# Two blocks of a 2048-wide model on one Trainium2 core: gate and up products with tokens stationary

## The chip, the core and the metric

The program runs on one core of one Trainium2 chip. The metric is the device time of one execution, in microseconds (us). Before the change the median of three runs is 2844.01 us (2843.94 to 2844.36). The core's engines work side by side, each through its own list of instructions in order, and wait for each other by semaphores: TensorE (matrix products, called PE in the profile; its weight loads are PEld), VectorE (DVE), ScalarE (ACT), GpSimd (POOL), and SyncE (SP), whose queue issues the transfers of weights.

## The reference

Two residual blocks follow each other, for 256 tokens of 2048 features, all in float32. The first has a modulation computed from a vector, a mixer with sliding-window attention and a gated linear recurrence, and a feed-forward layer. The second has gated linear attention and a feed-forward layer. What matters here are the two feed-forward layers, with 5632 hidden features:

```python
# first block
h2 = modulate(rms_norm(x, norm2_g[l]), sh2, sc2)
gate, up = jnp.split(h2 @ w_ffn_in[l], 2, axis=-1)
x = x + g2 * ((jax.nn.silu(gate) * up) @ w_ffn_out[l])
...
# second block
def swiglu(h, w_gu, w_down):
    g, u = jnp.split(h @ w_gu, 2, axis=-1)
    return (jax.nn.silu(g) * u) @ w_down
...
x = x + swiglu(rms_norm_2(x, norm_g[i, 1]), ffn_w_gu[i], ffn_w_down[i])
```

## The kernel before

Activations live in SBUF with features on the 128 partitions and the 256 tokens along the free axis: a tile of four feature tiles is `[128, 4, 256]`, a "slot" of 4 KB a partition, of which there are 24. The weights stream through once. A chunk is 1 MB: four k-tiles of 128 rows by 512 columns. `split` (L137) loads it on SP's queue into one of three `raw` buffers and makes, for two k-tiles at a time, a high part on ScalarE (L145, a copy to the rounded type float32r) and a low part on VectorE (L147, the difference); three buffers each hold such halves. The activations are kept as pairs of high and low parts in the same way (`split_act`, `normed`, `gained`). A product in nearly full precision is then the sum of three products: high by high, high by low, low by high.

`accumulate` (L151) does one chunk. In its usual form the weights are stationary: for each of four k-tiles and four feature tiles, three products (L169, L171, L173) with a 128x128 weight tile as the stationary operand and 256 tokens moving, 48 to a chunk; the result has features on partitions, in two PSUM banks of 512 columns. With `tokens=True` the activations are stationary: for each of four k-tiles and two token tiles, three products (L162 to L164) with a 128x128 piece of the activations stationary and 512 weight columns moving, 24 to a chunk; the result has tokens on partitions, one bank for each token tile. Before the change this second form serves the values of the attention (group 13) and those of the linear attention (`gvps`). PSUM has eight banks, handed out by the `bank` function in turn of need.

A feed-forward layer (`swiglu`, L614) works in two halves of 6 and 5 groups of 512 hidden features. For each group j: the gate product (four chunks, banks `fgps`), SiLU into a slot `sg`; then the up product (four chunks, banks `fups`), multiplied on VectorE with `sg`; then `split_act` of this into the pair `hid`. When the half is done, four groups of output features (`fops`) take the hidden pairs as moving operands, five or six chunks each, and `update` adds the result to x. In the first layer group 0 of the gate starts from `gx`, which lacks the norm's factor of each token; the factor is multiplied in after the product, and the share of the modulation's shift, `fb`, is a vector of 512 computed ahead by `matvec` (products on VectorE, a sum over partitions by four one-column products on TensorE, L226) and used as SiLU's bias. In the second layer all groups start from products without that factor: VectorE multiplies the gate by it before SiLU and again after SiLU (for the up part), L899 and L903.

The order of the work: the code is a list in which loads, conversions and products stand one behind the other, and work beside the weight stream stands in tasks (`spawn`) that go on at each `pump()`, between chunks. The conversions of chunks are marked as more urgent than what surrounds them. A scheduler takes this list with its data dependencies, and fixes for each engine an order in which an instruction goes to the engine when it is ready by the scheduler's own estimate, the one that stands earlier (or is more urgent) first. On the chip each engine keeps this order and waits where an input isn't there yet.

Of the kernel before, what the change touches and what calls it, by code (L numbers as in the profile page):

```python
# [18 lines left out]
P = 128  # L19
# [30 lines left out]
def block_pair_kernel(ctx: ExitStack, tc: tile.TileContext, a: dict):  # L50
# [20 lines left out]

    def halves(t):
        return [t[:, 0:2, :], t[:, 2:4, :]]

# [21 lines left out]
    # A task is a generator; it resumes between chunks, after as many as it yields.  # L96
# [40 lines left out]
    def split(ap):  # L137
        """hi + lo == the chunk, two k-tiles at a time."""
# [12 lines left out]
    def accumulate(ps, ap, src, first, last, tokens=False):  # L151
        """One chunk of four k-tiles by 512 features into two banks."""
        parts = split(ap)
        xh, xl = src
        for kk in range(4):
# [3 lines left out]
            if tokens:  # L159
                for t in range(2):  # L160
                    tsl = slice(t * P, (t + 1) * P)
                    nc.tensor.matmul(ps[t], xh[:, kk, tsl], hi[:, wk, :], start=fst, stop=False)  # L162
                    nc.tensor.matmul(ps[t], xh[:, kk, tsl], lo[:, wk, :], start=False, stop=False)
                    nc.tensor.matmul(ps[t], xl[:, kk, tsl], hi[:, wk, :], start=False, stop=lst)  # L164
                continue
            for f in range(4):
                wsl = slice(f * P, (f + 1) * P)
                o = ps[f // 2][:, f % 2, :]
                nc.tensor.matmul(o, hi[:, wk, wsl], xh[:, kk, :], start=fst and f % 2 == 0,  # L169
                                 stop=False, skip_group_check=True)  # L170
                nc.tensor.matmul(o, hi[:, wk, wsl], xl[:, kk, :], start=False, stop=False,  # L171
                                 skip_group_check=True)
                nc.tensor.matmul(o, lo[:, wk, wsl], xh[:, kk, :], start=False, stop=lst,  # L173
# [20 lines left out]
    def split_act(src, name):  # L194
        hi = slot(name + "h", F32R)
        nc.scalar.activation(hi, src, AF.Copy)
        lo = slot(name + "l", F32R)
        nc.vector.tensor_tensor(lo, src, f32(hi), ALU.subtract)
        return hi, lo

# [5 lines left out]
    def matvec(srcs, col, width, done, queue=nc.gpsimd):  # L206
        """Steps of vector @ width columns; srcs[k]: the rows of the vector's k-th 128 elements."""
# [14 lines left out]
        def reduce():  # L222
            n = width // P
            ps = bank("mvp")
            for f in range(n):
                nc.tensor.matmul(ps[:, f:f + 1], state["acc"][:, f * P:(f + 1) * P],  # L226
                                 ones[:, 0:1], start=True, stop=True)
            done(ps[:, 0:n])
# [51 lines left out]
    def normed(g, gain, inv, shift, name):  # L280
        t = slot(name + "t")
        hi = slot(name + "h", F32R)
        lo = slot(name + "l", F32R)
        for f in range(4):
# [4 lines left out]
            nc.scalar.activation(hi[:, f, :], t[:, f, :], AF.Identity, bias=sh)  # L289
            nc.vector.scalar_tensor_tensor(lo[:, f, :], t[:, f, :], sh, f32(hi[:, f, :]),  # L290
                                           ALU.add, ALU.subtract)
        return hi, lo

    def gained(g, gain, name):
        """hi, lo of gain * x; the norm's per-token factor is applied after the product."""
        hi = slot(name + "h", F32R)
        lo = slot(name + "l", F32R)
        for f in range(4):
            gj = gain[:, 4 * g + f:4 * g + f + 1]
            nc.scalar.activation(hi[:, f, :], x[g][:, f, :], AF.Copy, scale=gj)  # L300
            nc.vector.scalar_tensor_tensor(lo[:, f, :], x[g][:, f, :], gj, f32(hi[:, f, :]),
                                           ALU.mult, ALU.subtract)
        return hi, lo
# [4 lines left out]
    # ======================== first block ====================================  # L308
# [12 lines left out]
    def attend(g, q):  # L321
# [52 lines left out]
        yh = slot("yah", F32R)  # L374
        yl = slot("yal", F32R)
        for b, o in ((0, o0), (1, o1)):
            sl = slice(b * P, (b + 1) * P)
            nc.scalar.activation(yh[:, :, sl], o, AF.Copy)
            nc.vector.tensor_tensor(yl[:, :, sl], o, f32(yh[:, :, sl]), ALU.subtract)
        y_attn[g] = (yh, yl)  # L380

# [29 lines left out]
    # groups that keep their banks over all of k, and groups summed up in a slot  # L411
# [78 lines left out]
    # decay constant of the recurrence: -8 softplus(-lambda)  # L490
# [25 lines left out]
    def recur(g, ups):  # L516
# [30 lines left out]
        # 1 - a^2 = (1 + a^2) tanh(-log a)  # L547
# [45 lines left out]
    # the shift's share of the first gate group, whose norm factor comes after the product  # L593
    fb = const.tile([P, 4], F32, name="fb")
# [418 lines left out]
```

## Time and profile before

The profiled execution spans 2842.5 us from its first to its last instruction; a run's time also holds what lies around the span.

| | before |
|---|---|
| median of three runs | 2844.01 us |
| span of the profiled execution | 2842.5 us |
| TensorE busy | 2795.1 us (98%) |
| VectorE busy | 1815.7 us (64%) |
| ScalarE busy | 1313.2 us (46%) |
| granted TensorE clock, mean | 1.000 |
| HBM read | 597.06 MB, 211 GB/s over the span |

How to read it: busy time is the time in which at least one instruction of the engine was under way. Products on TensorE overlap: one lasts longer than the distance to the start of the next. A group's row has the line, engine, operation, the tiles written and read, their shapes, the count, then busy us, mean ns of one, and the idle time of the engine just before them with what ended it. A row of the timeline has start and duration in us, engine, line, operation and count. A row of the waits has who waited for whom, the total, the times and the longest. A row of windows has the stretch, its length, then busy us and instructions for each engine shown, the granted clock, the share of the DMA engines and GB/s.

### The profile page before, as it was taken

Reading aid. Unit: us, or ns where it says so; the run is one execution under the profiler, and the core shown is the slowest. Engines: PE = TensorE matmul, PEld = TensorE weight load, DVE = VectorE, ACT = ScalarE, POOL = GpSimd, SP = SyncE. Lnnn points to the kernel's source line nnn. Section 1 sums busy time; section 2 is a strip of 40 time slices with the busy share of each in tenths; the row PEclk is TensorE's granted clock in tenths of the full one; section 3 lists DMA queues with packets and bytes.
Section 4 is the critical chain, followed back from the end, with each engine's and each line's share of the span. In section 5 each row is a group of like instructions: output and inputs, shape, how many; then the busy total and the mean of one; then the engine's idle time right before and its main releaser. Section 6 shows DMA issues by size and latency. Waiting matters only on the chain.

```text
span 2842.5 us, 52147 instructions
## 1 busy us (share of the span) xinstructions
PE 2795.1 (98%) x22662; PEld 2760.6 (97%) x22662; DVE 1815.7 (64%) x1998; ACT 1313.2 (46%) x1481; POOL 25.7 (1%) x52
## 2 busy tenths in 40 slices
PE   4999999999999999999999999999999999999999
PEld 4999999999999999999999999899999999999999
DVE  8887866977777865444444667866655554455554
ACT  3446438763445444333444545555444443334333
POOL 1100000000000000000000000000000000000000
PEclk9999999999999999999999999999999999999999
DMA  9974784868875865555555544444555555555554
GB/s 370 353 298 143 279 294 171 289 221 319 327 261 181 295 251 187 180 187 178 185 187 179 182 168 163 148 146 166 178 182 189 179 182 189 178 183 188 178 190 151
DMA packets 100198, 602.54 MB, mean 212 GB/s; under 512 B 11120, under 2 KB 11632, under 8 KB 40576
## 3 DMA queue, kind: packets, MB, share of 16 engines
q1 hardware_dynamic: 93056, 574.03, 57.1%
q0 software_dynamic: 6912, 25.17, 2.2%
q8 instruction: 177, 2.90, 0.4%
q14 instruction: 53, 0.43, 0.0%
HBM read 597.06 MB, written 2.10 MB: 211 GB/s over the span
## 4 chain that ended last, share of the span: by engine, by line
PE 98%; DVE 1%; issue 0%; ACT 0%; DMA 0%; SPq 0%; DVEq 0%
PE fups L169 6%; PE fgps L169 6%; PE fops L173 6%; PE fops L171 6%; PE fops L169 6%; PE fups L173 6%; PE fups L171 6%; PE fgps L173 6%; PE fgps L171 6%; PE part L169 2%; PE part L171 2%; PE part L173 2%; PE aops L169 1%; PE glps L169 1%; PE ups L169 1%; PE wops L169 1%
## 5 line engine op out<-in xcount | busy, mean ns | idle before, releaser
L147 DVE TENSOR_TENSOR lo<-raw,hi 128x1024 fp32r<-128x1024 f32 x928 | 1135.1, 1223 | 937.9 <-ACT hi L145 936.3
L145 ACT ACTIVATE hi<-raw 128x1024 fp32r<-128x1024 f32 x928 | 980.9, 1057 | 1389.5 <-PE fops L171 292.7
L169 PE MATMUL fups<-hh,hi 128*128 128x256 f32 x1408 | 398.5, 283 | 0.0
L173 PE MATMUL fups<-hh,lo 128*128 128x256 f32 x1408 | 398.5, 283 | 0.0
L169 PE MATMUL fops<-hidh,hi 128*128 128x256 f32 x1408 | 398.5, 283 | 0.0
L171 PE MATMUL fops<-hidl,hi 128*128 128x256 f32 x1408 | 398.5, 283 | 0.0
L173 PE MATMUL fops<-hidh,lo 128*128 128x256 f32 x1408 | 398.5, 283 | 0.0
L171 PE MATMUL fups<-hl,hi 128*128 128x256 f32 x1408 | 398.5, 283 | 0.0
L169 PE MATMUL fgps<-hh,hi 128*128 128x256 f32 x1344 | 380.6, 283 | 0.0
L173 PE MATMUL fgps<-hh,lo 128*128 128x256 f32 x1344 | 380.3, 283 | 0.0
L171 PE MATMUL fgps<-hl,hi 128*128 128x256 f32 x1344 | 380.3, 283 | 0.0
L171 PEld LDWEIGHTS fups<-hl,hi 128*128 128x128 f32 x1408 | 270.3, 192 | 0.0
L169 PEld LDWEIGHTS fops<-hidh,hi 128*128 128x128 f32 x1408 | 270.3, 192 | 0.0
L171 PEld LDWEIGHTS fops<-hidl,hi 128*128 128x128 f32 x1408 | 270.3, 192 | 0.0
L173 PEld LDWEIGHTS fops<-hidh,lo 128*128 128x128 f32 x1408 | 270.3, 192 | 0.0
L169 PEld LDWEIGHTS fups<-hh,hi 128*128 128x128 f32 x1408 | 270.3, 192 | 0.0
L173 PEld LDWEIGHTS fups<-hh,lo 128*128 128x128 f32 x1408 | 270.3, 192 | 0.0
L171 PEld LDWEIGHTS fgps<-hl,hi 128*128 128x128 f32 x1344 | 258.0, 192 | 0.0
L169 PEld LDWEIGHTS fgps<-hh,hi 128*128 128x128 f32 x1344 | 258.0, 192 | 0.0
L173 PEld LDWEIGHTS fgps<-hh,lo 128*128 128x128 f32 x1344 | 258.0, 192 | 0.0
L218 DVE SCALAR_TENSOR_TENSOR mva<-mvw,cact,mva 128x1024 f32<-128x1024 f32 x180 | 230.3, 1280 | 14.2 <-DMA mvw<-ada_w 12.5
L169 PE MATMUL part<-hh,hi 128*128 128x256 f32 x512 | 147.3, 288 | 0.0
(319 smaller groups left out, 5511.7 us busy)
## 6 DMA issues: line engine op xcount, KB each, us to landing
raw<-w_in SPq DMA_DIRECT2D x88, 1024.0 KB, 5.0
raw<-w_ffn_in SPq DMA_DIRECT2D x88, 1024.0 KB, 4.9
raw<-ffn_w_gu SPq DMA_DIRECT2D x88, 1024.0 KB, 4.9
mvw<-ada_w SPq DMA_DIRECT2D x144, 512.0 KB, 6.8
raw<-gla_w_in SPq DMA_DIRECT2D x48, 1024.0 KB, 4.9
raw<-w_ffn_out SPq DMA_DIRECT2D x44, 1024.0 KB, 4.9
raw<-ffn_w_down SPq DMA_DIRECT2D x44, 1024.0 KB, 4.9
mvw<-ada_w POOLq DMA_DIRECT2D x48, 512.0 KB, 8.2
```

The costliest lines, as they stand in the source:

```text
L145: nc.scalar.activation(hi, rb, AF.Copy)
L147: nc.vector.tensor_tensor(lo, rb, f32(hi), ALU.subtract)
L169: nc.tensor.matmul(o, hi[:, wk, wsl], xh[:, kk, :], start=fst and f % 2 == 0, stop=False, skip_group_check=True)
L171: nc.tensor.matmul(o, hi[:, wk, wsl], xl[:, kk, :], start=False, stop=False, skip_group_check=True)
L173: nc.tensor.matmul(o, lo[:, wk, wsl], xh[:, kk, :], start=False, stop=lst, skip_group_check=True)
L218: nc.vector.scalar_tensor_tensor(state["acc"], w, col(k), state["acc"], ALU.mult, ALU.add)
```

## The change

Gate and up products of both layers take the second form of `accumulate`: `project(..., True)`, with tokens stationary. Their results stand with tokens on partitions, so SiLU and the product with up work on `[128 tokens, 2, 512]`, and the norm's factor becomes a scalar of each partition: `by_token` transposes the row of factors and keeps one column for each token tile. In the second layer SiLU takes that factor as its scale, and the factor of the up part goes into the product of the two; in the first layer's group 0 the factor and the shift row `fb` (now `[128, 512]`, the same on all partitions, made by one 512-column product with a matrix of ones) are applied by one VectorE instruction for each token tile. The output products `fops` still need hidden features on partitions, so the task `turned` transposes the product on TensorE, eight 128x128 transposes for each group into two banks `tps`, and makes the high and low part from there. The task is spawned behind the up group with a delay that lets it go on at the very next `pump()`.

Pairs become a class: two tiles `[128, 2, 2, 256]`, each with high and low part of two feature tiles, in place of one tile of high and one of low parts; `split_act` and the attention's output write them in halves. This holds for every stage. The rest of the diff takes out comments.

```diff
+    class Pair:
+        def __init__(self, name):
+            self.t = [slot(name, F32R, [P, 2, 2, T]) for _ in range(2)]
...
+        def hi(self, kk):
+            return self.t[kk // 2][:, kk % 2, 0, :]
+        def lo(self, kk):
+            return self.t[kk // 2][:, kk % 2, 1, :]
+        def his(self, b):
+            return self.t[b][:, :, 0, :]
+        def los(self, b):
+            return self.t[b][:, :, 1, :]
...
     def split_act(src, name):
-        hi = slot(name + "h", F32R)
-        nc.scalar.activation(hi, src, AF.Copy)
-        lo = slot(name + "l", F32R)
-        nc.vector.tensor_tensor(lo, src, f32(hi), ALU.subtract)
-        return hi, lo
+        p = Pair(name)
+        for b, part in enumerate(halves(src)):
+            nc.scalar.activation(p.his(b), part, AF.Copy)
+            nc.vector.tensor_tensor(p.los(b), part, f32(p.his(b)), ALU.subtract)
+        return p
...
             ps = bank("mvp")
+            if row:
+                nc.tensor.matmul(ps[:, 0:width], ones, state["acc"], start=True, stop=True)
+                done(ps[:, 0:width])
+                return
...
+    def by_token(inv, name):
+        out = small.tile([P, 2], F32, tag="invp", name=name)
+        ps = bank("tokps", [P, T])
+        for t in range(2):
+            nc.tensor.transpose(ps[:, t * P:(t + 1) * P], inv[:, t * P:(t + 1) * P], ident)
+            nc.vector.tensor_copy(out[:, t:t + 1], ps[:, t * P:t * P + 1])
+        return out
...
-    fb = const.tile([P, 4], F32, name="fb")
+    fb = slot("fb", shape=[P, 512])
...
+    def turned(sv):
+        p = Pair("hid")
+        yield p
+        for b in range(2):
+            tp = bank("tps", [P, 2, T])
+            for i in range(2):
+                f = 2 * b + i
+                for t in range(2):
+                    nc.tensor.transpose(tp[:, i, t * P:(t + 1) * P], sv[:, t, f * P:(f + 1) * P],
+                                        ident)
+            nc.scalar.activation(p.his(b), tp, AF.Copy)
+            nc.vector.tensor_tensor(p.los(b), tp, f32(p.his(b)), ALU.subtract)
+
     def swiglu(w_in, w_out, gate, up, update):
         for n, half in enumerate((range(0, 6), range(6, FG))):
-            hid = []
+            hid, turns = [], []
             for j in half:
                 sg = gate(j)
                 pump()
-                hid.append(up(sg, j))
+                gen = turned(up(sg, j))
+                hid.append(next(gen))
+                turns.append(spawn(gen, 1))
                 pump()
             for f in range(NG):
-                update(n, f, project(chunks_of(w_out, f, list(half)), hid, "fops"))
+                chunks = chunks_of(w_out, f, list(half))
+                ps = banks("fops")
+                for c in range(len(chunks)):
+                    finish(turns[c])
+                    accumulate(ps, chunks[c], hid[c], c == 0, c == len(chunks) - 1)
+                    if c < len(chunks) - 1:
+                        pump()
+                update(n, f, ps)
                 pump()
...
+        norm2["invp"] = by_token(norm2["inv"], "invp2")
...
     def gate1(j):
-        sg = slot("sg")
-        ps = project(chunks_of("w_ffn_in", j), gx if j == 0 else h2, "fgps")
+        sg = slot("sg", shape=[P, 2, 512])
+        ps = project(chunks_of("w_ffn_in", j), gx if j == 0 else h2, "fgps", True)
         if j == 0:
             finish(norm_task)
-            for b, part in enumerate(halves(sg)):
-                nc.vector.tensor_tensor(part, ps[b], pair(norm2["inv"]), ALU.mult)
-            for f in range(4):
-                nc.scalar.activation(sg[:, f, :], sg[:, f, :], AF.Silu, bias=fb[:, f:f + 1])
+            for t in range(2):
+                nc.vector.scalar_tensor_tensor(sg[:, t, :], ps[t], norm2["invp"][:, t:t + 1],
+                                               fb, ALU.mult, ALU.add)
+            nc.scalar.activation(sg, sg, AF.Silu)
         else:
...
     def up1(sg, j):
-        ps = project(chunks_of("w_ffn_in", FG + j), h2, "fups")
-        for b, part in enumerate(halves(sg)):
-            nc.vector.tensor_tensor(part, ps[b], part, ALU.mult)
-        return split_act(sg, "hid")
+        ps = project(chunks_of("w_ffn_in", FG + j), h2, "fups", True)
+        for t in range(2):
+            nc.vector.tensor_tensor(sg[:, t, :], ps[t], sg[:, t, :], ALU.mult)
+        return sg
...
     def gate2(j):
-        sg = slot("sg")
-        ps = project(chunks_of("ffn_w_gu", j), h2, "fgps")
+        sg = slot("sg", shape=[P, 2, 512])
+        ps = project(chunks_of("ffn_w_gu", j), h2, "fgps", True)
         finish(norm_task)
-        for b, part in enumerate(halves(sg)):
-            nc.vector.tensor_tensor(part, ps[b], norm5["inv"], ALU.mult)
-        sv = slot("sv")
-        nc.scalar.activation(sv, sg, AF.Silu)
-        for b, part in enumerate(halves(sv)):
-            nc.vector.tensor_tensor(part, part, norm5["inv"], ALU.mult)
-        return sv
+        for t in range(2):
+            nc.scalar.activation(sg[:, t, :], ps[t], AF.Silu, scale=norm5["inv"][:, t:t + 1])
+        return sg
 
     def up2(sg, j):
-        ps = project(chunks_of("ffn_w_gu", FG + j), h2, "fups")
-        for b, part in enumerate(halves(sg)):
-            nc.vector.tensor_tensor(part, ps[b], part, ALU.mult)
-        return split_act(sg, "hid")
+        ps = project(chunks_of("ffn_w_gu", FG + j), h2, "fups", True)
+        for t in range(2):
+            nc.vector.scalar_tensor_tensor(sg[:, t, :], ps[t], norm5["inv"][:, t:t + 1],
+                                           sg[:, t, :], ALU.mult, ALU.mult)
+        return sg
```

More of the change, by code (lines that the diff above doesn't have):

```diff
@@ L70, in f32, with both @@
         return ap.bitcast(F32)
+    class Pair:
+        def __init__(self, name):
+            self.t = [slot(name, F32R, [P, 2, 2, T]) for _ in range(2)]
+        def both(self, kk):
+            return self.t[kk // 2][:, kk % 2, :, :]
+        def hi(self, kk):
[6 more added lines that the diff above has]
+            return self.t[b][:, :, 1, :]
     def halves(t):
@@ L168, in accumulate @@
                 o = ps[f // 2][:, f % 2, :]
-                nc.tensor.matmul(o, hi[:, wk, wsl], xh[:, kk, :], start=fst and f % 2 == 0,
+                nc.tensor.matmul(o, hi[:, wk, wsl], src.hi(kk), start=fst and f % 2 == 0,
                                  stop=False, skip_group_check=True)
-                nc.tensor.matmul(o, hi[:, wk, wsl], xl[:, kk, :], start=False, stop=False,
+                nc.tensor.matmul(o, hi[:, wk, wsl], src.lo(kk), start=False, stop=False,
                                  skip_group_check=True)
-                nc.tensor.matmul(o, lo[:, wk, wsl], xh[:, kk, :], start=False, stop=lst,
+                nc.tensor.matmul(o, lo[:, wk, wsl], src.hi(kk), start=False, stop=lst,
                                  skip_group_check=True)
@@ L204, in block_pair_kernel, with matvec @@
     mod = const.tile([P, 96], F32, name="mod")
-    def matvec(srcs, col, width, done, queue=nc.gpsimd):
+    def matvec(srcs, col, width, done, queue=nc.gpsimd, row=False):
         state = {}
@@ L373, in attend @@
         nc.tensor.matmul(o1, vn[:, 1, vg], p1[:, 1, :], start=False, stop=True)
-        yh = slot("yah", F32R)
-        yl = slot("yal", F32R)
+        y = Pair("ya")
         for b, o in ((0, o0), (1, o1)):
             sl = slice(b * P, (b + 1) * P)
-            nc.scalar.activation(yh[:, :, sl], o, AF.Copy)
-            nc.vector.tensor_tensor(yl[:, :, sl], o, f32(yh[:, :, sl]), ALU.subtract)
-        y_attn[g] = (yh, yl)
+            for w in range(2):
+                ow = o[:, 2 * w:2 * w + 2, :]
+                nc.scalar.activation(y.his(w)[:, :, sl], ow, AF.Copy)
+                nc.vector.tensor_tensor(y.los(w)[:, :, sl], ow, f32(y.his(w)[:, :, sl]),
+                                        ALU.subtract)
+        y_attn[g] = y
     gain1 = const.tile([P, 16], F32, name="gain1")
@@ L683, in block_pair_kernel @@
     tok = const.tile([P, T], F32, name="tok")
-    tokp = const.tile([P, 2], F32, name="tokp")
+    tokp = []
     tokb = pair(tok)
@@ L696, in two_norms @@
         yield 1
-        ps = bank("tokps", [P, T])
-        for t in range(2):
-            nc.tensor.transpose(ps[:, t * P:(t + 1) * P], tok[:, t * P:(t + 1) * P], ident)
-            nc.vector.tensor_copy(tokp[:, t:t + 1], ps[:, t * P:t * P + 1])
+        tokp.append(by_token(tok, "tokp"))
         for g in range(NG):
@@ L727, in decays @@
         for k in range(NK):
-            xh, xl = h[k // 4]
-            kk = k % 4
-            nc.tensor.matmul(ps, warh[:, k, :], xh[:, kk, :], start=k == 0, stop=False)
-            nc.tensor.matmul(ps, warh[:, k, :], xl[:, kk, :], start=False, stop=False)
-            nc.tensor.matmul(ps, warl[:, k, :], xh[:, kk, :], start=False, stop=k == NK - 1)
+            hk, kk = h[k // 4], k % 4
+            nc.tensor.matmul(ps, warh[:, k, :], hk.hi(kk), start=k == 0, stop=False)
+            nc.tensor.matmul(ps, warh[:, k, :], hk.lo(kk), start=False, stop=False)
+            nc.tensor.matmul(ps, warl[:, k, :], hk.hi(kk), start=False, stop=k == NK - 1)
         alr = small.tile([16, T], F32, tag="alr", name="alr", bufs=1)
@@ L823, in block_pair_kernel @@
         for t in range(2):
-            nc.scalar.activation(vg[:, t, :], ps[t], AF.Copy, scale=tokp[:, t:t + 1])
+            nc.scalar.activation(vg[:, t, :], ps[t], AF.Copy, scale=tokp[0][:, t:t + 1])
         vt.append(vg)
```

36 lines of the change are left out of this document (18 added, 18 removed).

## The prediction

> **What bounds the kernel now.** I read the page first: busy shares, and the chain that ended last by engine.
>
> ```profile
> span 2842.5 us, 52147 instructions
> PE 2795.1 (98%) x22662; PEld 2760.6 (97%) x22662; DVE 1815.7 (64%) x1998; ACT 1313.2 (46%) x1481; POOL 25.7 (1%) x52
> ...
> PE 98%; DVE 1%; issue 0%; ACT 0%; DMA 0%; SPq 0%; DVEq 0%
> ```
>
> TensorE is busy through the span and is 98% of the chain (the windows below show its granted clock as 1.00). Then the waits, of TensorE alone:
>
> ```profile
> PE mvp L226 <- DVE mva L218: 34.4, 1, 34.4
> PE e L169 <- ACT hh L289: 4.4, 1, 4.4
> ...
> PE gkps L173 <- DVE lo L147: 1.4, 3, 0.9
> ```
>
> These are the first two and the last of five lines, in falling order: 34.4 us at the start, under 10 elsewhere, and not one line of either feed-forward layer. So the time is the sum over TensorE's instructions of the distance from one start to the next, and only what changes that sum, or makes TensorE wait, counts. A busy TensorE says nothing of how fast it goes, so I take distances between starts, not durations, which overlap.
>
> Which products the change touches, from the groups by form:
>
> ```profile
> L169 PE MATMUL fgps<-hh,hi 128*128 128x256 f32 x1344 | 380.6, 283 | 0.0
> L169 PE MATMUL fgps<-gxh,hi 128*128 128x256 f32 x64 | 18.3, 286 | 0.0
> L169 PE MATMUL fups<-hh,hi 128*128 128x256 f32 x1408 | 398.5, 283 | 0.0
> ```
>
> 1344 + 64 + 1408 = 2816 on L169, and as many on L171 and on L173: 8448 products of 256 columns, in 176 chunks of 48 (88 of gate, 88 of up).
>
> **The products themselves.** Their pace, from a window of the second layer that holds only such products, and from the timeline's first and last start in it:
>
> ```profile
> 2400.00:2500.00 100.00, 100.00 (x836) 1.00 0.53 181
> ```
>
> ```profile
> 2399.74 0.28 PE L169 MATMUL fops<-hidh,hi 128*128 128x256 f32 x1
> ...
> 2499.94 0.28 PE L171 MATMUL fgps<-hl,hi 128*128 128x256 f32 x1
> ```
>
> 100.20 us over 835 steps: 120.0 ns each, 5.760 us a chunk. The kernel already has the form that replaces them, the value groups of the linear attention (gvps: tokens stationary, 512 weight columns moving, same types). A window there and its timeline:
>
> ```profile
> 1773.80:1783.80 10.00, 10.00 (x45) 1.00 0.44 171
> ```
>
> ```profile
> 1773.60 0.39 PE L164 MATMUL gvps<-hi,hl 128*128 128x512 f32 x1
> ...
> 1783.58 0.39 PE L163 MATMUL gvps<-lo,hh 128*128 128x512 f32 x1
> ```
>
> 44 steps in 9.98 us: 226.8 ns each. A chunk becomes 24 of these, 5.443 us. That saves 0.317 us a chunk (13.2 ns for each two short products put together), and over 176 chunks **55.8 us**. A chunk's form does not depend on which stage it stands in, so I take this without a discount.
>
> **The transposes.** Each of the 22 groups (11 in each layer) gets 8 transposes of 128x128 float32. The attention's transposes are the same instruction: first their duration (shortest, median, longest), then their pace in the chain (start, time on it, count), with a row for later use. The timeline of the level products (lps, xps) between value chunks shows what a burst in a stream of long products costs:
>
> ```profile
> L365 PE MATMUL tp<-ident,s x48: 270/272/328, 240.1 to 322.9; 128*128 128x128 f32 x48
> ```
>
> ```profile
> 240.30 1.31 PE tp L365 x12
> 1152.48 1.68 PE mvp L226 x16
> ```
>
> ```profile
> 1784.03 1.95 PE L793 MATMUL lps<-qe,ke 128*128 128x128 f32 x16
> 1785.82 1.06 PE L785 MATMUL xps<-qe,ke 128*128 128x128 f32 x8
> ...
> 1786.94 0.40 PE L163 MATMUL gvps<-lo,hh 128*128 128x512 f32 x1
> ```
>
> 12 transposes take 1.31 us, 0.109 each. The burst of 24, the way back into long products included (1786.94 is the start of the second of these), takes 1786.94 - 0.227 - 1784.03 = 2.68 us, 0.112 each, so going in and out of a burst costs next to nothing. 176 x 0.111 = **+19.5 us**, all of it on the path, since TensorE has no idle time to hide it in.
>
> The Trainium skill prices a transpose differently: the page "TensorE: Matmul & The Clock Gate", section "Part 4: PE-mode transpose", has about 275 ns for one in a kernel. The trace agrees as to the duration (272 ns) but not as to the pace (109); with 275 ns at each step the 176 would cost an estimated 48 us, and the whole change would gain an estimated 4. This is the third rival.
>
> **The wait for them.** In the code the transposes of group j stand right behind the product on VectorE that makes their input, ahead of gate group j+1. In that order TensorE would stop, with the whole next gate group queued behind it. Rows at the end of an up group:
>
> ```profile
> 2538.54 1.41 DVE L909 TENSOR_TENSOR sv<-fups,sv 128x512 f32<-128x512 f32 x2
> ...
> 2538.94 0.28 PE L173 MATMUL fups<-hh,lo 128*128 128x256 f32 x1
> ...
> 2539.06 0.28 PE L169 MATMUL fgps<-hh,hi 128*128 128x256 f32 x1
> ...
> 2539.14 1.06 ACT L145 ACTIVATE hi<-raw 128x1024 fp32r<-128x1024 f32 x1 [1.82 <-PE fups L171]
> ...
> 2540.23 1.23 DVE L147 TENSOR_TENSOR lo<-raw,hi 128x1024 fp32r<-128x1024 f32 x1 [0.28 <-ACT hi L145]
> ```
>
> VectorE ends 2539.95 - 2539.06 = 0.9 us after TensorE could go on; one such wait in each group is 22 x 0.9 = 19.8 us, the upper bound. The lower bound is none: the scheduler may let the next gate chunk, whose weights lie ready, go ahead. The nearest row decides, two transposes that stand in one piece of code with a copy on VectorE between them:
>
> ```profile
> 1679.85 0.28 PE L173 MATMUL gkps<-hh,lo 128*128 128x256 f32 x1
> 1679.97 0.27 PE L699 MATMUL tokps<-ident,tok 128*128 128x128 f32 x1
> 1680.00 0.36 PE L730 MATMUL lrps<-hh,warh 128*16 128x256 f32 x1
> 1680.20 0.28 PE L731 MATMUL lrps<-hl,warh 128*16 128x256 f32 x1
> ...
> 1682.31 0.28 PE L731 MATMUL lrps<-hl,warh 128*16 128x256 f32 x1
> 1682.50 0.33 PE L699 MATMUL tokps<-ident,tok 128*128 128x128 f32 x1
> 1682.78 0.28 PE L730 MATMUL lrps<-hh,warh 128*16 128x256 f32 x1
> ```
>
> ```profile
> 1682.29 0.15 DVE L700 COPY tokp<-tokps 128x1 f32<-128x1 f32 x1
> ```
>
> Between the two, 2.5 us of other products ran: the order is by readiness, not by the text. The first cost 1680.20 - 1679.85 - 2 x 0.12 = 0.11 us; the second, placed right where its copy ended (1682.44), stands with one lrps product between the last two starts: 0.47 - 2 x 0.117 = 0.24, thus 0.13 too much. I expect two bursts a group (token tile 0, then 1) and half of that excess each: 22 x 0.13 = **+2.9 us**.
>
> **Norm factors and the shift row.** Two norms get two transposes each more (4 x 0.11 to 0.24: **+0.7 us**; the pair for the linear attention stays). The shift's share becomes one 512-column float32 product in place of four with one column; 16 narrow ones take 1.68 us in the chain above, so four 0.42; a wide one lies between the 0.23 of a gvps step and four 128-column float32 products, 0.45. That is -0.2 to 0; I take 0. The first layer's normed tiles must not become late; rows of the first one's last step and of its first use (the first of the two starts):
>
> ```profile
> 908.30 0.48 DVE L290 SCALAR_TENSOR_TENSOR hl<-ht,mod,hh 128x256 fp32r<-128x256 f32 x1
> ```
>
> ```profile
> L169 PE MATMUL fups<-hh,hi x1408: 283/283/363, 914.4 to 2723.0; 128*128 128x256 f32 x176
> ```
>
> It was done at 908.78 and used at 914.4. Of these 5.6 us, gate group 0, shorter by four chunks, takes 1.3 and the new copies (0.15 each, above) 0.3: no wait.
>
> **What VectorE and ScalarE do instead.** Second layer:
>
> ```profile
> 2080.00:2730.00 650.00, 650.00 (x5416) 649.89 (x5416) 340.84 (x317) 263.69 (x253) 0.00 (x0) 1.00 0.53 183
> ```
>
> ```profile
> L909 DVE TENSOR_TENSOR sv<-fups,sv 128x512 f32<-128x512 f32 x22 | 15.2, 692 | 0.3
> L198 DVE TENSOR_TENSOR hidl<-sv,hidh 128x1024 fp32r<-128x1024 f32 x11 | 13.4, 1219 | 0.0
> ```
>
> VectorE is busy 341 of 650 us, ScalarE 264. In the second layer a group loses on VectorE four scalings by the norm factor (L899, L903; by the equal shape of L909 some 0.69 each), and in both its low part costs two PSUM reads of 0.69 in place of the 1.22 of L198: 2.6 us less in the second layer, 0.2 more in the first. ScalarE gains a few tenths a group. Cutting the pairs elsewhere into halves and quarters adds some tenths at some 16 places. All of it is hidden by products that run meanwhile; uncovered, those 16 places would cost about 5 us. No DMA is added or moved: SP's queue carries the same chunks in the same order. The 24 slots are filled as before (8 normed, 12 hidden, one or two gates and a modulation sum), and 8 banks hold two each of up, next gate, next up and transposes.
>
> **The sum:** -55.8 + 19.5 + 2.9 + 0.7 = -32.7 us. The span of 2842.5 becomes 2809.8. The three runs have a median of 2844.0, 1.5 above the span, for what lies around it; that does not change: **2811.3 us**, 1.1% less. Its own range, from no wait at all to half of the upper bound: 2808 to 2818.
>
> **Rivals.**
> 1. *TensorE stands still for the transposes* (the text's order is kept): 19.8 in place of 2.9, **2828**. For: in the code nothing stands between. Against: the tokps rows. 11%.
> 2. *The low part of the weights comes late*, **slower**. VectorE takes its instructions in order, and the hidden tile's low part now waits for ScalarE, which waits for the transposes; a weight half (L147) behind it waits too. Three halves are held, so one is made two ahead: from the release at 2539.06 the rows hi and lo of that timeline run to 2541.46, 2.4 us, and the use is two halves, 24 x 0.227 = 5.4 us, away. VectorE must be held up 3.0 us beyond its own work before TensorE notices, and 32.7 / 22 = 1.5 us more in each group to eat the gain; held 5.2 us a group, it gives -32.7 + 22 x 2.2 = +15.7, **2860**. For: gkps waited for lo three times. Against: 0.9 us was the longest, and the hidden pair of before (L198) was such a chain without any wait of TensorE. 5%.
> 3. *A transpose's full duration shows*, as where each waits for its own input: 176 x 0.272 = 47.9 in place of 19.5, **2840**, no difference that can be measured. Against: the pace of 0.109. 3%.
> 4. *Two short products cost no more than one long one*, so that nothing is saved and the transposes are paid: 2844.0 + 23.1 = **2867**, slower. Against: 226.8 beside 240.0 in one execution. 2%.
>
> The Trainium skill speaks for the fourth: the same page's "Back-to-back issue gap" has N/2.4 + 2.5 ns, a saving of only 2.5 ns for each pair, an estimated 10.6 us, less than the transposes cost. The trace disagrees on both widths (120.0 where the formula has 109, 226.8 where it has 216).
>
> **Numbers.** The forecast has 79%. The range of 2804 to 2829 holds it and the first rival, and a few us below for bounds I took too high. Faster by over 0.2% (5.7 us, about what a measurement of this kernel tells from none) are the forecast and the first rival: 0.90; within: the third, 0.03; slower: the second and fourth, 0.07.
>
> **What would show it.** fgps and fups products 128x512, 1408 on each of three lines, 227 ns apart; if 240, rival 4. 176 transposes to tps, mostly four or more in a row 0.11 apart, between products of the next gate group; if alone and far apart, rival 3. TensorE's waits: no line with tps above some 5 us; about 20 from VectorE's sg is rival 1; a line with lo L147 of tens of us is rival 2. The granted clock stays 1.00; if it fell, every distance here would be wrong.

## The result, and the profile after

The changed kernel takes 2779.05 us (median of four runs, 2775.35 to 2779.31), the kernel before beside it 2844.19 (2843.94 to 2844.75). The ratio is 0.9768, with a 95% interval of 0.9754 to 0.9781: 65.1 us faster, twice the 32.7 us forecast, and below the range of 2804 to 2829.

The page of the profile after (its own run took 2775.35 us), first the busy shares and then the chain that ended last by engine:

```profile
span 2773.6 us, 43912 instructions
PE 2710.8 (98%) x18612; PEld 2489.2 (90%) x18612; DVE 1784.8 (64%) x2000; ACT 1321.3 (48%) x1531; POOL 25.7 (1%) x52
...
PE 91%; DVE 5%; ACT 1%; issue 1%; DMA 1%; SPq 0%; DVEq 0%; ACTq 0%
```

TensorE still fills the span, with 4050 instructions fewer: 8448 short products became 4224 long ones, 176 transposes came in addition, and the small changes (four transposes of norm factors more, six instructions of `mvp` fewer) make up the rest. The chain now passes over VectorE in places, and the waits of TensorE (who waited for whom, us in total, times, longest) show how much that is worth:

```profile
PE mvp L251 <- DVE mva L239: 36.7, 3, 34.4
PE e L189 <- ACT h L313: 4.4, 1, 4.4
PE tps L658 <- DVE sg L716: 3.6, 11, 0.8
PE tps L658 <- DVE sg L961: 3.6, 11, 0.3
PE tp L397 <- DVE s L389: 2.9, 2, 1.9
PE gkps L193 <- DVE lo L167: 2.3, 3, 0.9
```

These are the first six of 13 lines. The two with `tps` are new, 7.2 us in 22 stops. So no wait explains the gain; it must lie in the pace of the products. The groups of the changed products, and the new transposes (shortest, median, longest, first and last start):

```profile
L184 PE MATMUL fups<-hi,h 128*128 128x512 f32 x704 | 276.7, 393 | 0.0
L182 PE MATMUL fgps<-hi,h 128*128 128x512 f32 x672 | 264.6, 394 | 0.0
```

```profile
L658 PE MATMUL tps<-ident,sg x176: 270/272/332, 920.6 to 2661.3; 128*128 128x128 f32 x176
```

The change did what it says. Then I summed the distances from each start on TensorE to the next, by the tile written, over both traces. The table has all that differs by 0.5 us or more:

| tile written | before, us | after, us | difference |
|---|---|---|---|
| fgps, fups, tps (gate, up, transposes) | 1014.25 | 1000.17 | -14.1 |
| fops (output products, not touched) | 510.79 | 483.43 | -27.4 |
| ggps, grps, gps, ups, part, aops, gqps, glps, lops, wops, gkps (not touched) | | | -32.7 |
| tp, gvps, e | | | +4.1 |
| whole span | 2842.49 | 2773.56 | -68.9 |

Where the change was made, it gained less than half of what I forecast. The other 60 us come from products that it does not touch. Windows of the trace after show it (stretch, length, TensorE busy with its instructions, granted clock, DMA share, GB/s):

```profile
620.00:660.00 40.00, 40.00 (x342) 1.00 0.89 338
2310.00:2430.00 120.00, 120.00 (x1062) 1.00 0.56 194
```

A window counts every instruction that overlaps it, so it holds one duration (0.28 us) more than its length: 40.28 / 342 = 117.8 ns from start to start in the first, which holds `lops` and `glps`, and 120.28 / 1062 = 113.3 ns in the second, `fops`. Before, every such product took 120.0, at the same granted clock of 1.00. The question of the experiments was why.

### The profile page after: what moved, and what is told of

Same layout as the page of the kernel before. It is cut to its first block, busy times and chain, and to the rows that moved or that the text cites. A ratio compares the mean times of both kernels' runs of the same rounds, so it can differ in the third digit from the quotient of the medians.

```text
span 2773.6 us, 43912 instructions
## 1 busy us (share of the span) xinstructions
PE 2710.8 (98%) x18612; PEld 2489.2 (90%) x18612; DVE 1784.8 (64%) x2000; ACT 1321.3 (48%) x1531; POOL 25.7 (1%) x52
## 4 chain that ended last, share of the span: by engine, by line
PE 91%; DVE 5%; ACT 1%; issue 1%; DMA 1%; SPq 0%; DVEq 0%; ACTq 0%
PE fops L189 6%; PE fops L191 6%; PE fops L193 6%; PE fgps L184 6%; PE fgps L183 6%; PE fgps L182 6%; PE fups L184 5%; PE fups L183 5%; PE fups L182 5%; DVE lo L167 2%; PE part L189 2%; PE part L191 2%; PE part L193 2%; DVE mva L239 1%; DMA mvw<-ada_w 1%
## 5 line engine op out<-in xcount | busy, mean ns | idle before, releaser
L189 PE MATMUL fops<-hid,hi 128*128 128x256 f32 x1408 | 389.0, 276 | 0.0
L193 PE MATMUL fops<-hid,lo 128*128 128x256 f32 x1408 | 388.8, 276 | 0.0
L191 PE MATMUL fops<-hid,hi 128*128 128x256 f32 x1408 | 388.8, 276 | 0.0
L183 PE MATMUL fups<-lo,h 128*128 128x512 f32 x704 | 275.9, 392 | 0.9 <-DVE lo L167 0.9
L184 PE MATMUL fups<-hi,h 128*128 128x512 f32 x704 | 276.7, 393 | 0.0
L182 PE MATMUL fups<-hi,h 128*128 128x512 f32 x704 | 274.2, 390 | 0.0
L184 PE MATMUL fgps<-hi,h 128*128 128x512 f32 x672 | 264.9, 394 | 0.0
L182 PE MATMUL fgps<-hi,h 128*128 128x512 f32 x672 | 264.6, 394 | 0.0
L191 PEld LDWEIGHTS fops<-hid,hi 128*128 128x128 f32 x1408 | 264.3, 188 | 0.0
L189 PEld LDWEIGHTS fops<-hid,hi 128*128 128x128 f32 x1408 | 264.3, 188 | 0.0
L193 PEld LDWEIGHTS fops<-hid,lo 128*128 128x128 f32 x1408 | 264.3, 188 | 0.0
L183 PE MATMUL fgps<-lo,h 128*128 128x512 f32 x672 | 263.3, 392 | 0.0
L182 PEld LDWEIGHTS fups<-hi,h 128*128 128x128 f32 x704 | 132.2, 188 | 29.3
L184 PEld LDWEIGHTS fups<-hi,h 128*128 128x128 f32 x704 | 132.3, 188 | 27.4
L183 PEld LDWEIGHTS fgps<-lo,h 128*128 128x128 f32 x672 | 126.3, 188 | 27.4
L182 PEld LDWEIGHTS fgps<-hi,h 128*128 128x128 f32 x672 | 126.3, 188 | 26.3
L184 PEld LDWEIGHTS fgps<-hi,h 128*128 128x128 f32 x672 | 126.3, 188 | 26.0
```

Source lines behind the costliest of these rows:

```text
L182: nc.tensor.matmul(ps[t], xh, hi[:, wk, :], start=fst, stop=False)
L183: nc.tensor.matmul(ps[t], xh, lo[:, wk, :], start=False, stop=False)
L184: nc.tensor.matmul(ps[t], xl, hi[:, wk, :], start=False, stop=lst)
L189: nc.tensor.matmul(o, hi[:, wk, wsl], src.hi(kk), start=fst and f % 2 == 0, stop=False, skip_group_check=True)
L191: nc.tensor.matmul(o, hi[:, wk, wsl], src.lo(kk), start=False, stop=False, skip_group_check=True)
L193: nc.tensor.matmul(o, lo[:, wk, wsl], src.hi(kk), start=False, stop=lst, skip_group_check=True)
```

## The experiments

Two things differ for every stage, and each made a theory.

*Layout.* The pairs are laid out in another way (class `Pair`): high and low part of two feature tiles lie side by side in one tile.

*Place.* The constants lost two small tiles (`fb` is now a slot, the linear attention's token factors stand in `small`). So the slots begin 64 bytes a partition earlier, and the buffers of `small` behind them grew by as much, which leaves the weight buffers where they were. Slots and weight buffers are 4096 bytes long, and every operand of a product begins at a multiple of 512 bytes inside its buffer; all activations thus share one remainder of their start modulo 256, and all weights another. I call "distance" the start of the slots minus that of the weight buffers, modulo 256 bytes. By the built programs it is 0 before (both at remainder 128) and 192 after (slots at 64). In the short form the slots hold the moving operand and the weight buffers the stationary one; in the long form it is the other way round.

**Each kernel with the other's place.** Unused tiles ahead of the slots and behind them move the slots alone. Kernel before, moved to distance 192:

```diff
+    pad1 = ctx.enter_context(tc.tile_pool(name="pad1", bufs=1))
+    nc.gpsimd.memset(pad1.tile([P, 48], F32, name="pad1"), 0.0)
     act = ctx.enter_context(tc.tile_pool(name="act", bufs=SLOTS))
+    pad2 = ctx.enter_context(tc.tile_pool(name="pad2", bufs=1))
+    nc.gpsimd.memset(pad2.tile([P, 16], F32, name="pad2"), 0.0)
```

> The kernel before, with its 24 slots 192 bytes further on, so that they start 64 bytes past a multiple of 256, as after the change, in place of 128; all that lies behind the slots (weights' raw, high and low parts) keeps its place within 256 bytes. Nothing else differs. If the pace of the short products is set by where the slots start (place), the 21,228 steps between short products fall from 120.0 ns to 113 to 118 and the run takes 2705 to 2800 us, likeliest 2730. If it is set by high and low part standing side by side in one tile (layout), the step stays at 120.0 and the run at 2844.

The changed kernel, moved back to distance 0, has the same lines with 16 ahead and 48 behind:

> The changed kernel, with its slots 64 bytes further on, 128 past a multiple of 256, as before the change; what lies behind them keeps its place within 256 bytes but for small tiles. Place: short products back at 120.0 ns, long ones at 227 in place of 229; 12,742 x 5.5 ns more and 4,700 x 2.2 less, 2835 to 2840 us. Layout: steps of 113 to 118 as in the changed kernel, 2779.

Measured: the kernel before, moved, 2756.24 us (2753.32 to 2757.91; ratio to the kernel before 0.9689, 0.9675 to 0.9703). The changed kernel, moved back, 2825.62 us (2825.52 to 2826.58; ratio 0.9935, 0.9919 to 0.9952). Windows of short products in the former, then in the latter; the latter's second window holds long products:

```profile
2290.00:2410.00 120.00, 120.00 (x1062) 1.00 0.57 193
```

```profile
2350.00:2470.00 120.00, 120.00 (x1002) 1.00 0.54 181
...
2170.00:2202.00 32.00, 32.00 (x143) 1.00 0.56 189
```

120.28 / 1062 = 113.3 ns without any `Pair`, and 120.28 / 1002 = 120.0 with it: the layout falls, the place decides. The first time lies in the range of "place", above its likeliest 2730. The second lies below the 2835 to 2840 us that "place" gave: it took 5.5 ns for each short product, and by the traces of the kernel after and of this one they became 4.8 slower on average. In the moved-back kernel the slots lie where they did before the change and the weight buffers 256 bytes further on (by the built programs), and the pace is 120.0 as before, so 256 bytes more between the two make no difference. At distance 0 the long products take (32.00 + 0.39) / 143 = 0.2265 us, the 226.8 ns of the prediction to within one in the count. At distance 192 they are slower; the kernel after has

```profile
2125.00:2165.00 40.00, 40.00 (x177) 1.00 0.53 184
```

40.39 / 177 = 0.2282, and by single starts over the stage 229.0 ns. So the place helps the short form and harms the long one. The four kernels, with the change down and the place across:

| | distance 0 | distance 192 |
|---|---|---|
| products as before | 2844.2 | 2756.2 |
| products changed | 2825.6 | 2779.05 |
| effect of the change | -18.6 | +22.8 |

At distance 192 the change is a loss. There the gate and up products take 974.4 us in short form (115.3 ns each) and 971.4 in long form: 3.0 us saved, against some 28.8 for the transposes and the stops around them. The +22.8 holds something else too: the output products, the same in both kernels, took 8.6 us less in the changed one (479.4 against 488.0), for at this distance there are two paces. In the moved kernel the window above has the fast one; an earlier one with the same products (`fops`) has 120.28 / 1021 = 117.8 ns:

```profile
1160.00:1280.00 120.00, 120.00 (x1021) 1.00 0.55 187
```

**All places, in turn.** If only equal remainders were bad, buffers spread over all places would nearly all be good. Slots and weight buffers 32 bytes longer than before, so that their starts go round, in the kernel before and then in the changed one:

```diff
+    nc.gpsimd.memset(act.tile([P, 1032], F32, tag="a", name="wide")[:, 0:1], 0.0)
+    nc.gpsimd.memset(hip.tile([P, 1032], F32, tag="hi", name="wideh")[:, 0:1], 0.0)
+    nc.gpsimd.memset(lop.tile([P, 1032], F32, tag="lo", name="widel")[:, 0:1], 0.0)
```

> The kernel before, with 32 bytes more in each slot and in each buffer of the weights' high and low parts, so that tiles start at all eight multiples of 32 within 256 bytes. Place: the step between short products differs by the places of the operands, 120.0 where the activations lie as before and less elsewhere. Layout: 120.0 throughout, 2844 us.

> The changed kernel, spread in the same way. Place: the steps of short and of long products differ by the places of their operands, which shows the best place for each. Layout: 113 to 118 and 229 as in the changed kernel, whatever the place.

Measured, one run each: 2812.59 and 2827.57 us. Short products take some 118.3 ns in the one and 118.4 in the other, long ones some 231.7 in both. So a spread is no cure. The paces lie between the extremes that single distances show below, as an average over good and bad places would; the pace at each place was not taken from these two runs.

**Single distances.** The lines of the first experiment in the kernel before, with 8 and 56, 16 and 48, 32 and 32, 40 and 24, 56 and 8 elements ahead and behind: distances of 32, 64, 128, 160 and 224 bytes.

> The kernel before, slots 32 bytes further on, the weights' buffers at the same place within 256 bytes. The distance of a slot's start from a weight buffer's start, within 256 bytes, was 0 before (120.0 ns a short product), and 192 after the change and in the first move (113 to 118). If it is only the meeting of equal places that costs (clash), every other distance gives 113 to 118 ns, 2740 to 2800 us. If the cost falls off with distance (graded), 32 lies between: 116 to 120, 2780 to 2844 us.

> As the last, 64 bytes further on (64 the other way round from the first move). Clash: 113 to 118 ns, 2740 to 2800 us. Graded: like the first move, 2756 us. If the place counts within 128 bytes only, the same as 192, 2756 us.

> As the last, 128 bytes further on. If the place counts within 128 bytes only, this is no move: 120.0 ns, 2844 us. Within 256 and clash or graded: 113 to 118 ns, 2740 to 2790 us.

> The same with 160 bytes (96 the other way). Smooth: between 128 and 192, 2765 to 2825 us. Symmetric says nothing of it. If places that are an odd number of 32 bytes apart go like 32 (116.7 ns): 2790.

> The kernel before, slots 224 bytes further on (32 the other way). Distances 0, 32, 64, 128 and 192 gave 2844, 2790, 2799, 2826 and 2756 us. If a distance and its opposite do alike (symmetric), this is like 32: 116 to 118 ns, 2785 to 2795 us. If it goes smoothly round 256 bytes (smooth), it lies between 0 and 192: 2765 to 2835.

Measured, one run each but for distances 0 and 192; the paces by single starts, in the stages of `fops` (short) and `gvps` (long):

| distance, bytes | time, us | short, ns | long, ns |
|---|---|---|---|
| 0 | 2844.2 | 120.0 | 226.8 |
| 32 | 2790.47 | 116.7 | 233.3 |
| 64 | 2798.70 | 117.8 | 233.3 |
| 128 | 2825.66 | 118.7 | 232.2 |
| 160 | 2818.76 | 118.7 | 233.3 |
| 192 | 2756.24 | 113.3 and 117.8 | 229.0 |
| 224 | 2815.18 | 118.3 | 233.3 |

Windows of `fops` at 32 and at 128:

```profile
2315.00:2435.00 120.00, 120.00 (x1031) 1.00 0.56 191
```

```profile
2350.00:2470.00 120.00, 120.00 (x1013) 1.00 0.54 187
```

120.28 / 1031 = 116.7 and 120.28 / 1013 = 118.7. Distance 128 is not like distance 0, most clearly for the long form (232.2 and 226.8), so the period is not 128 bytes. "Clash" fails at 128, 160 and 224, which are all above 2800 us, and "graded" at 64, which is not like 192. "Symmetric" fails at 224, which is not like 32. The wide ranges of "smooth" hold the times at 160 and 224, but the time falls by 63 us from 160 to 192 and rises by 59 from there to 224. I have no rule for the order. By the times of these runs 0 is the worst place for the short form and 192 the best; for the long form 0 is the best, 192 next, and the rest cost 2 to 3% more.

The table's paces of short products are those of one stage. Elsewhere in the same runs other paces stand at the same distance: 117.8 ns in `glps` at 32, 119.9 there at 128, 117.3 in most of `ups` at 160. At 64 an up group of the first layer has 20.28 / 179 = 113.3, the fast pace of 192:

```profile
902.00:922.00 20.00, 20.00 (x179) 1.00 0.59 202
```

So 64 and 192 share both paces and differ in how many products have the fast one. At 0 (120.0) and at 224 (118.3) `fops`, `fups`, `fgps`, `ups` and `glps` all go at one pace.

**Which places count.** Is it the slots' own start, or their start against the weights? Everything moved by 192 bytes (the first experiment without its second tile), distance again 0:

> The kernel before, with everything from the slots on moved by 192 bytes: slots, small tiles, modulation strips and the weights' raw, high and low parts. Slots start where they do in the first move, but their distance from the weights is 0 as before. If the distance counts (relative), 120.0 ns and 2844 us. If the slots' own place counts (absolute), 113 to 118 ns and 2756.

Measured 2848.29 us, and the window has 120.28 / 1002 = 120.0 ns:

```profile
2365.00:2485.00 120.00, 120.00 (x1002) 1.00 0.54 185
```

The time is 4 us above the kernel before, but the pace is its pace. It is the start of the one against the other that counts. Then 64 bytes ahead of the buffers of the high parts and 192 ahead of those of the low parts, so that the high parts alone move; and 64 bytes ahead of the low parts alone:

```diff
+    pad1 = ctx.enter_context(tc.tile_pool(name="pad1", bufs=1))
+    nc.gpsimd.memset(pad1.tile([P, 16], F32, name="pad1"), 0.0)
     hip = ctx.enter_context(tc.tile_pool(name="hip", bufs=HIS))
+    pad2 = ctx.enter_context(tc.tile_pool(name="pad2", bufs=1))
+    nc.gpsimd.memset(pad2.tile([P, 48], F32, name="pad2"), 0.0)
     lop = ctx.enter_context(tc.tile_pool(name="lop", bufs=LOS))
```

> The kernel before, with the three buffers of the weights' high parts alone 64 bytes further on (slots at distance 192 from them, at 0 from the low parts). Of three short products in a row (high by high, high by low, low by high) two have a high part as weights. If each product pays for its own weights and tokens (own), or for the weights that are loaded while it streams (next), two of three steps fall to 113 to 118 ns and the mean to 115.5 to 119, 2770 to 2825 us; own: L173's step stays longest; next: L171's. If all operands that are in use together count (all), one pace for all three, above 118.

> The same with the low parts' buffers alone moved. Own or next: one of three steps falls, the mean to 117.8 to 119.3, 2795 to 2830 us; own: L173's step is the short one; next: L171's. All: one pace for all three, as with the high parts moved.

Measured 2807.63 and 2805.19 us, one run each. Had each product gone by its own pair of buffers, two of three products would have changed in the first and one of three in the second. All three changed in both: by single starts in `fops` the three steps are 117.5, 118.3 and 117.5 ns with the high parts moved and 117.5, 117.5 and 118.3 with the low parts moved, 117.8 in the mean of either. A window of the former, 120.28 / 1022 = 117.7:

```profile
2335.00:2455.00 120.00, 120.00 (x1022) 1.00 0.55 189
```

By "own" and "next" one or two of the three steps had to stay at 120.0, so both fail; "all", one pace for all three, comes nearest, with a pace a little lower than it said. The weight loads of `fops`, by line (high by high, high by low, low by high), show more; first with the high parts moved, then with the low parts:

```profile
L173 PEld LDWEIGHTS fops<-hidh,hi x1408: 188/188/188, 1159.4 to 2801.5; 128*128 128x128 f32 x176
...
L175 PEld LDWEIGHTS fops<-hidl,hi x1408: 192/192/192, 1159.6 to 2801.6; 128*128 128x128 f32 x176
...
L177 PEld LDWEIGHTS fops<-hidh,lo x1408: 187/188/188, 1159.7 to 2801.7; 128*128 128x128 f32 x176
```

```profile
L171 PEld LDWEIGHTS fops<-hidh,hi x1408: 187/188/188, 1157.5 to 2799.1; 128*128 128x128 f32 x176
...
L173 PEld LDWEIGHTS fops<-hidl,hi x1408: 188/188/188, 1157.6 to 2799.2; 128*128 128x128 f32 x176
...
L175 PEld LDWEIGHTS fops<-hidh,lo x1408: 192/192/192, 1157.7 to 2799.3; 128*128 128x128 f32 x176
```

One load in three takes 192 ns, the others 188. With the high parts moved it is the second of the two loads from them, with the low parts moved the one from those; the loads from the buffers that stayed at distance 0 became short. At distance 0 all three take 192, in the kernel before as with everything moved; one of the three rows from the page before (busy us, mean ns):

```profile
L169 PEld LDWEIGHTS fops<-hidh,hi 128*128 128x128 f32 x1408 | 270.3, 192 | 0.0
```

So a load does not go by its own distance alone. In these runs and at 192 three paces thus belong to three, one or none of the long loads: 120.0, 117.8 and 113.3 ns. This counting fails at all the other distances, where the median of every load of `fops` is 187 or 188 and the pace 116.7 to 118.7.

**The waits for the transposes.** The timeline of the kernel after at the end of an up group (start, duration, engine, line, operation, tiles, count, idle time before with its releaser):

```profile
2120.02 0.40 PE L184 MATMUL fups<-hi,h 128*128 128x512 f32 x1
2120.74 0.44 PE L658 MATMUL tps<-ident,sg 128*128 128x128 f32 x2 [0.32 <-DVE sg L961]
2120.94 0.48 PE L182 MATMUL fgps<-hi,h 128*128 128x512 f32 x1
...
2121.49 0.39 PE L184 MATMUL fgps<-hi,h 128*128 128x512 f32 x1
2121.72 0.82 PE L658 MATMUL tps<-ident,sg 128*128 128x128 f32 x6
2122.29 0.48 PE L182 MATMUL fgps<-hi,h 128*128 128x512 f32 x1
```

TensorE does stop: 0.72 us from the last up product to the first transpose, where 0.23 would do. It takes two transposes, three gate products, and then the other six. To price this alone, at distance 0, the transposes of the moved-back kernel are released one `pump()` later, behind the first chunk of the next gate group:

```diff
-                turns.append(spawn(gen, 1))
+                turns.append(spawn(gen, 2))
```

> The changed kernel with its slots back at the old place (2825.6 us), and the task of the transposes spawned with delay 2 in place of 1, so that it goes on one chunk later, when its input is long done. If TensorE's 8 us of waits for VectorE's sg, with what they carry (some 0.57 us between two starts in each of 22 groups), come from placing the transposes too early (wait), these lines go, and the run gets 8 to 13 us shorter, 2813 to 2818. If the eight transposes cost what they cost whenever they run (price), it stays at 2823 to 2827.

Measured 2812.69 us (2810.20 to 2814.17; ratio to the kernel before 0.9890, 0.9874 to 0.9907), 12.9 less than without it, as "wait" said. The timeline and the waits:

```profile
2111.27 0.40 PE L188 MATMUL fgps<-hi,h 128*128 128x512 f32 x1
2111.51 1.04 PE L662 MATMUL tps<-ident,sg 128*128 128x128 f32 x8
2112.30 0.48 PE L186 MATMUL fgps<-hi,h 128*128 128x512 f32 x1
```

```profile
PE mvp L255 <- DVE mva L243: 34.9, 1, 34.9
PE e L193 <- ACT h L317: 4.4, 1, 4.4
PE tp L401 <- DVE s L393: 2.0, 2, 1.0
```

Eight transposes in a row and, in all six lines of the waits, of which these are the first three, none with `tps`. Over the trace the transposes with what they hold up cost some 18.2 us here and 29.5 in the moved-back kernel: about 11.3 us of pure waiting. How the steps beside a burst are counted moves the two sums by up to 3 us, their difference by one or two.

The same edit in the changed kernel as it stands, distance 192:

> The changed kernel as it is (slots at distance 192) with the transposes one chunk later. If waits and place add up (sum), the 12.9 us that this saved at the old place are saved here too: 2779 - 13 = 2766 us, still more than the kernel before with moved slots, 2756. If the place's gain hangs on the transposes (linked), it comes out above 2772 or below 2760.

Measured 2787.88 us (2786.95 to 2788.84; ratio to the kernel before 0.9800, 0.9784 to 0.9816): 8.8 us slower than the changed kernel. The waits for `tps` are gone here too, but the short output products lost their fast pace. A window of `fops`, and the loads of its three lines:

```profile
2325.00:2435.00 110.00, 110.00 (x937) 1.00 0.56 189
```

```profile
L189 PEld LDWEIGHTS fops<-hid,hi x1408: 187/188/190, 1152.4 to 2780.8; 128*128 128x128 f32 x176
...
L191 PEld LDWEIGHTS fops<-hid,hi x1408: 187/192/192, 1152.6 to 2780.9; 128*128 128x128 f32 x176
...
L193 PEld LDWEIGHTS fops<-hid,lo x1408: 187/188/188, 1152.7 to 2781.0; 128*128 128x128 f32 x176
```

110.28 / 937 = 117.7 ns, and again one load in three is a long one. 4224 products by 117.7 - 113.5 ns are some 17.7 us lost, about 10.7 of waiting are won (28.8 to some 18.1, as at distance 0), and TensorE waits 2.6 us more for the low part of weights in the attention's output products: +9.6, where 8.8 was measured. So "sum" fails and "linked" holds. The trace shows where the pace changed:

```profile
1153.06 0.28 PE L191 MATMUL fops<-hid,hi 128*128 128x256 f32 x1
...
1157.94 0.28 PE L193 MATMUL fops<-hid,lo 128*128 128x256 f32 x1
1158.05 1.04 PE L658 MATMUL tps<-ident,sg 128*128 128x128 f32 x8
1158.85 0.36 PE L189 MATMUL fops<-hid,hi 128*128 128x256 f32 x1
```

The first chunk of `fops` goes at the fast pace (4.88 us over 43 steps, 113.5 ns); then the delayed transposes of the last group break the stream, and all that follows goes at 117.8. This is so at each of the four starts of `fops`. In the changed kernel the transposes come within the first few of these products, and what follows goes at 113.3. The distance is 192 in both.

**The fastest version.** The kernel before with its slots moved by 64 bytes (192 ahead is 64 back, modulo 256) and nothing else runs in 2756.24 us. That beats both kernels, and no product is changed for it.

## Why the prediction was wrong

The sign was right, with some luck: at distance 0, where the paces were read, the change gains 18.6 us, but at the distance where the changed kernel stands it costs 22.8, and the gain there is that of a shift nobody had planned. The size came from something that the sum left out. By its own steps:

- *The products, -55.8.* Right at the place it was read from: 226.8 beside 120.0 ns. The moved-back kernel gains some 52.4 us in the gate and up products (1014.25 - (991.40 - 29.5), by distances between starts), the one with late transposes 54.2. In the kernel as changed, it failed: 229.0 ns, and what it is compared with depends on the place too.
- *"A chunk's form does not depend on which stage it stands in, so I take this without a discount"* is true of stages at distance 0 (120.0 in all of them), but the step behind it failed: that both paces are properties of the form. And *"the 24 slots are filled as before"* was true of their number and not of their address. I read the diff for instructions, waits and banks, and took the move of `fb` and of the token factors as costing nothing. These two lines shift the slots by 64 bytes, and a shift of this size is worth 88 us in the kernel before. **That is the failed step**: "only what changes that sum, or makes TensorE wait, counts" was applied to the products that the diff touches, with the durations of all others held fixed. 60 of the 68.9 us stand in that place.
- *The transposes, +19.5.* Right: 272 ns long, 0.11 us apart, some 18.2 us where nothing is waited for. The third rival shows in the duration only. The Trainium skill's price for a transpose ("TensorE: Matmul & The Clock Gate", "Part 4: PE-mode transpose", about 275 ns) agrees with the duration, not with the pace.
- *The wait for them, +2.9.* Mis-sized: 11.3 us by the trace, 12.9 by the medians, nearer to the first rival's 19.8. I took the scheduler's reordering from a row in which other products had been ready for 2.5 us. Here two or three products go ahead of the last six transposes only; the first two stand right behind the up group, and TensorE waits for their input with the next gate group queued behind.
- *Norm factors, shift row (+0.7), VectorE and ScalarE (0).* Nothing speaks against them: waits for a low part of weights stay at 0.4 to 2.3 us in the waits after, and the second rival did not occur. A wait of 2.6 us more in the first block's attention (`tp`) was not foreseen.
- *The fourth rival*, two short products no dearer than one long, is refuted at distance 0 and nearly true at 192 (230.6 for two, 229.0 for one). The Trainium skill's formula ("TensorE: Matmul & The Clock Gate", "Back-to-back issue gap"), which that section gives for an isolated product and by which a pair would save an estimated 2.5 ns, is near the 1.6 ns of that place and far from the 13.2 of the other.

With the place held at 0 and the stops removed, the kernel takes 2812.69 us, where the sum without its 2.9 of waiting gives 2808.4; the span of its profiled execution is 34.1 us shorter than before, where that sum has 35.6. The rest of the sum was sound to within a few us. As the kernel stands, two things of opposite signs were missing, 10 us more of waiting (12.9 where 2.9 stood) and 46.6 of place (2825.62 to 2779.05); the same few us are left.

## What to carry to other kernels

A tile added to or taken from a pool shifts every buffer behind it, and this can be worth more than the change itself: look at the start of the moving operand against that of the stationary one, before and after, and price a change of form with the place held fixed (a few unused bytes ahead and behind do that). When products that a diff does not touch change their pace, look for what moved, not for what was rewritten. A tuned place belongs to a form: the byte distance that is best for 256 moving columns is not the best one for 512.

## What the runs showed of the hardware

- The pace of back-to-back products at a granted clock of 1.00 depends on where the activations' buffers start against the weights', with a period of 256 bytes as far as tried (256 bytes more changed nothing at distance 0, 128 did): 113.3 to 120.0 ns for 256 columns of float32r (6%), 226.8 to 233.3 for 512 (3%). Best and worst places of the two forms are not the same. What in the hardware does this is open; no run here shows it.
- At one distance the short form can have more than one pace: 113.3 and 117.8 ns at 192 and at 64. At 192 each holds over hundreds of products and changes where the stream is broken; the windows of the kernel after have the first in `fops` and the second in `lops` and `glps`. Which one follows a break is open: transposes that came one chunk later left `fops` in the slower one.
- Open as well: why moving either the high or the low parts alone speeds up all three products; whether another distance (96 was not tried) is better still; and whether the two small tiles alone, moved in the kernel before, give the 2756 us. That was not run; the moved kernel has the same distance, made with unused tiles.
